# Mixer projections of a hybrid decoder trunk: high weights times both parts of the input in one 512-wide product, 256 columns at a time

## The chip, the cores and the metric

The kernel runs on one core of a Trainium2 chip. A core has a matrix engine (TensorE, PE in the profile, with its weight loads shown apart as PEld), a vector engine (VectorE, DVE), an engine for activations and copies (ScalarE, ACT), GpSimd (POOL) and SyncE (SP), which issues most DMAs here. The metric is the device time of one execution in microseconds. The time before is 1442.95 us, the median of three runs between 1440.83 and 1443.87 us.

## What is computed

Four pre-norm residual layers over a sequence of 256 positions, width 1024, in fp32. Each layer is a token mixer, an MLP with a squared ReLU and a gated projection of a per-layer input. Layers 0 and 3 mix by an S5 state space with a gated linear unit, layer 1 by forgetting attention (FoX), layer 2 by gated linear attention (GLA). Cut to the parts that matter here:

```python
# S5 (layers 0 and 3), after the scan
z = gelu(y) @ w_glu
z1, z2 = split(z, 2)                 # left gate, right gate
return (z1 * sigmoid(z2)) @ w_out
# FoX (layer 1)
proj = xn @ w_in                     # queries, keys, values (1024 each), 16 forget gates
o = softmax(q @ k.T * scale + forget_bias, causal) @ v
return o @ w_out
# GLA (layer 2)
proj = xn @ w_in                     # queries, keys (512 each), values, output gate r
o = chunked_linear_attention(q, k, v, gates)
return (norm(o) * gn_g * silu(r)) @ w_out
# every layer
h = h + mixer(rmsnorm(h))
h = h + square(relu(rmsnorm(h) @ w1)) @ w2
h = h + (p @ W_pp) * sigmoid(rmsnorm(h) @ W_pg)
```

## The kernel before

**Layout.** The residual stream lies transposed in SBUF, features on partitions and time along the row: `H[k]`, k = 0 to 7, each 128 x 256, two to a tile `HH[n]`. Weights stream from HBM once, in units of 512 KB.

**Two parts of each number.** A product is made from a high part (rounded to the fast format fp32r) and a low part (the rest) of both factors: high weights times high input, high weights times low input, low weights times high input. Inputs are kept as tiles of two row blocks, `x[k // 2][:, k % 2]`, with high and low part side by side, 256 columns each, so that both make one operand of 512 columns. `unit` (L187) loads raw weights (L171, three buffers), copies them into fp32r on ACT (`whi`, L179) and subtracts on DVE (`wlo`, L181), with four buffers for each part.

**Three ways to multiply.**
- `dense` (L202) takes 512 output columns at a time in two PSUM banks and goes through the input by units of 256 rows x 512 columns. `pairs` (L217) and `col` (L195) issue three products of 256 columns for each 128 x 128 block of weights: high x high, high x low, low x high (L198, L199, L200), all summed in the same 256 columns. One unit is 24 products. After four units the two banks are finished and handed to `evac`.
- `wide` (L226), used by the MLP, gives each 128 output columns a bank of its own: the high weights multiply both parts in one product of 512 columns (L234), the low weights the high part in one of 256 (L236). The bank then holds two halves, which `summed` (L241) adds: a copy of one half on ACT (L244) and an addition on DVE (L245).
- `rows` (L248) puts time on partitions, for the values of FoX and GLA and GLA's output gate.

**PSUM** has eight banks: three under the tag `acc`, three `wk`, one `po`, one `mk` (L22).

**Who uses dense.** FoX: queries (scaled by -0.125) and keys, for each half `cb` of the heads (L553, L554), both with `acc` alone; their `evac` (`augmented`, L511) multiplies with the row factor `r` straight from PSUM (L517). GLA: queries and keys (L632, L633); `query` multiplies PSUM into `e1`, `key` into `e2` and `e3`. S5: the left gate (L1106), whose `evac` multiplies with the sigmoid of the right gate (L1103) and splits the result into the two parts of `m`. `out_proj` (L293), the product by w_out at the end of each mixer, adds its banks to `HH[n]` (L296). Also the gate of the per-layer input (L473) and, through `pairs`, S5's right gate (L1253).

**What sets the order.** The program is written step by step, and the framework's scheduler (L1442) fixes the order on each engine when the program is built: it takes the earliest step in program order that its own timeline holds ready and for which a buffer is free. So PE's list interleaves steps: the attention parts of one half of FoX (scores L528, transposes L539, product with the values L548) stand among the queries and keys of the other half, and among the first units by w_out. Each engine then executes its list in order. In FoX, `o` has four tiles, one for each four heads (L565); in GLA four, two for each half of the value columns (L694).

Of the kernel before, what the change touches and what calls it, by code (L numbers as in the profile page):

```python
# [13 lines left out]
ALU = mybir.AluOpType  # L14
# [3 lines left out]
T, D, FF, DEPTH = 256, 1024, 4096, 4  # L18
# [42 lines left out]
class Trunk:  # L61
# [164 lines left out]
    def wide(self, ps, x, hi, lo, k, first, last):  # L226
# [3 lines left out]
        for n in range(4):  # L230
# [4 lines left out]
            for i in range(UK):  # L235
                self.last_mm = mm(ps[n][:, 0], lo[:, i, s], v[i][:, 0], start=False, stop=last and i == UK - 1, skip_group_check=True)  # L236

    def banks(self, tags):
        return [self.psum((128, 2, T), t) for t in tags]

# [52 lines left out]
    def out_proj(self, x, w):  # L293

        def evac(n, ps):
            self.nc.vector.tensor_tensor(self.HH[n], self.HH[n], ps, ALU.add)  # L296
        self.dense(x, w, evac, tags=("acc", "wk"))

    def log_sigmoid(self, *pairs):

# [188 lines left out]
    def fox(self, l):  # L489
        nc, A = self.nc, self.A  # L490
        NH, HD = 16, 64
        x = self.scaled(l)
        sq = self.squares()
        bf = self.small("bf", [NH, 1], bufs=1)
        self.load(bf, A["fox_bf"])
        f, e = (self.small(n, (NH, T), bufs=1) for n in ("w1", "w2"))
        rows = self.rstd_rows(sq)
        self.masks()
        r = self.rstd(rows)
        self.side(x, A["fox_wf"], f)  # L500
        nc.vector.tensor_tensor(f, f, r[0:NH], ALU.mult)
        nc.vector.tensor_scalar(f, f, bf, None, ALU.add)
        self.log_sigmoid((f, e))
        cf = self.a2("cf", (NH, 2, T))
        nc.gpsimd.memset(e, 1.0)
        nc.vector.tensor_tensor_scan(cf[:, 0], e, f, 0.0, ALU.mult, ALU.add)
        nc.vector.tensor_scalar(cf[:, 1], cf[:, 0], -1.0, None, ALU.mult)

        qk = [[self.t4("aug", (128, 2, 2, T)) for _ in range(4)] for i in range(2)]

        def augmented(i):  # L511
            def evac(n, ps):
                t = qk[i][n]
                nc.gpsimd.memset(t[HD:HD + 2], 1.0)
                nc.sync.dma_start(t[HD + 1 - i:HD + 2 - i].rearrange("x a b t -> x (a b) t"), cf[4 * n:4 * n + 4, 1 - i])
                for h in range(2):
                    nc.vector.tensor_tensor(t[0:HD, :, h], ps[h * HD:(h + 1) * HD], r[0:HD].unsqueeze(1).broadcast_to([HD, 2, T]), ALU.mult)  # L517
            return evac

        def weights(cb, half, heads):  # L520

            n, g = half + 1, len(heads)
            ps = self.psum((128, g, n * 128))
            m, z = self.small("m", [128, 4], bufs=3), self.small("z", [128, 4], bufs=3)
            s = self.t2("s", (128, g, n * 128))
            for i, h in enumerate(heads):
                q, k = (qk[j][cb * 2 + h // 4][0:HD + 2, h // 2 % 2, h % 2] for j in range(2))
                nc.tensor.matmul(ps[:, i], q[:, half * 128:(half + 1) * 128], k[:, :n * 128], start=True, stop=True)  # L528
            for i in range(g):
                nc.vector.tensor_tensor_reduce(s[:, i], ps[:, i], self.far[:, T - n * 128:], 1.0, 3.0e38, ALU.add, ALU.min, m[:, i:i + 1])  # L530
                nc.scalar.activation(s[:, i], s[:, i], AF.Exp, bias=m[:, i:i + 1], scale=-1.0, accum_out=z[:, i:i + 1])
            rz = self.small("rz", [128, 4], bufs=3)
            nc.vector.reciprocal(rz[:, :g], z[:, :g])
            for i in range(g):
                nc.vector.tensor_scalar(s[:, i], s[:, i], rz[:, i:i + 1], None, ALU.mult)
            pt = self.psum((128, g, n, 128), "mk")
            for i in range(g):
                for kb in range(n):
                    nc.tensor.transpose(pt[:, i, kb], s[:, i, kb * 128:(kb + 1) * 128], self.ident)  # L539
            pT = self.t2("pT", (128, g, n, 128))  # L540
            nc.scalar.copy(pT, pt)
            return pT

        def values(v, po, half, heads, pT):
            n = half + 1
            for kb in range(n):
                for i, h in enumerate(heads):
                    nc.tensor.matmul(po[(h % 2) * HD:(h % 2 + 1) * HD, h // 2 % 2, half * 128:(half + 1) * 128],  # L548
                                     v[:, kb, h * HD:(h + 1) * HD], pT[:, i, kb], start=kb == 0, stop=kb == n - 1)

        o = self.ktiles("o")
        for cb in range(2):
            self.dense(x, A["fox_w_in"][:, 0:D], augmented(0), (cb,), -0.125)  # L553
            self.dense(x, A["fox_w_in"][:, D:2 * D], augmented(1), (cb,))  # L554
            v = self.t4("v", (128, 2, 512), tag="c4")
            for quad in range(2):
                hs = list(range(quad * 4, quad * 4 + 4))
                parts = [(0, hs), (1, hs[:2]), (1, hs[2:])]
                pT = [weights(cb, *p) for p in parts]
                if quad == 0:  # L560
                    self.rows(x, A["fox_w_in"][:, 2 * D:], cb, lambda half, ps: nc.scalar.activation(v[:, half], ps, AF.Identity, scale=rows[:, half:half + 1]))
                po = self.psum((128, 2, T), "po")
                for i, p in enumerate(parts):
                    values(v, po, *p, pT[i])
                d = o[cb * 2 + quad]  # L565
                self.split(po, d[:, :, 0], d[:, :, 1])
        self.out_proj(o, A["fox_w_out"])

    def gla(self, l):
        nc, A = self.nc, self.A  # L570
        NH, DK, DV = 4, 128, 256
        x = self.scaled(l)
# [7 lines left out]
        rows = self.rstd_rows(sq)  # L580
        r = self.rstd(rows)
# [3 lines left out]
        y, e, cum = (self.t4(n, (128, NH, T)) for n in ("gy", "ge", "cum"))  # L585
        for h in range(NH):
            ps = self.psum((128, T))
# [13 lines left out]
        for h in range(NH):  # L601
            nc.scalar.activation(e1[:, h], cum[:, h], AF.Exp, scale=1.0 / 16.0)
            nc.scalar.activation(e2[:, h], cum[:, h], AF.Exp, scale=-1.0 / 16.0)
            c = slice(h, h + 1)
# [5 lines left out]
        v = [self.t4("v", (128, 2, 512), tag="c4") for half in range(2)]  # L610
        v = [[t[:, b] for b in range(2)] for t in v]
# [2 lines left out]

        def query(n, ps):
            e = e1[:, 2 * n:2 * n + 2]
            nc.vector.scalar_tensor_tensor(e, ps, DK ** -0.5, e, ALU.mult, ALU.mult)

        ku = [self.a2("ku") for _ in range(2)]

        def key(n, ps):
            n -= 2
            for e in (e2, e3):
                e = e[:, 2 * n:2 * n + 2]
                nc.vector.tensor_tensor(e, ps, e, ALU.mult)
            pt = self.psum((128, 2, 2, 128))
            for half in range(2):
                for i in range(2):
                    nc.tensor.transpose(pt[:, half, i], e3[:, 2 * n + i, half * 128:(half + 1) * 128], self.ident)
                nc.scalar.copy(ku[half].rearrange("p (h k) -> p h k", h=NH)[:, 2 * n:2 * n + 2], pt[:, half])  # L630

        self.dense(x, A["gla_w_in"], query, (0,))  # L632
        self.dense(x, A["gla_w_in"], key, (1,), tags=("acc", "wk"))  # L633
        state = [self.a2("state", (128, 2, DV)) for b in range(2)]
        os = [[None, None], [None, None]]
        att = []
# [11 lines left out]
        for half in range(2):  # L648
            at = att[half]
            for b in range(2):  # L650
                po = self.psum((128, 2, DV))
                for c in range(2):
# [4 lines left out]
                    for hh in range(2):  # L657
                        h = 2 * b + hh
# [6 lines left out]
                    for hh in range(2):  # L665
                        h = 2 * b + hh
                        nc.tensor.matmul(pu[:, hh, :], ku[half][cs, h * DK:(h + 1) * DK], v[half][b][cs, hh * DV:(hh + 1) * DV],
                                         start=True, stop=True)
# [421 lines left out]
    def s5(self, l):  # L1090
        nc, A = self.nc, self.A
        E = mybir.EngineType
        with nullcontext():
            steps = self.s5_start(l)
            with nullcontext():
                gT, last = steps()
        m = self.ktiles("glu", tag="m4")
        self.lo_after, self.raw_after = [last], self.last_unit
        for b, sg in enumerate(self.sg):

            def left(n, ps):
                t = sg[n % 2]
                nc.vector.tensor_tensor(t, ps, t, ALU.mult)  # L1103
                self.split(t, m[n][:, :, 0], m[n][:, :, 1])

            self.dense(gT, A["s5_w_glu"][l // 3], left, (b,), tags=("acc", "wk"))  # L1106
        self.lo_after, self.raw_after = [], None
        self.out_proj(m, A["s5_w_out"][l // 3])

# [336 lines left out]
```

## Time and profile before

| what | value |
|---|---|
| median of three runs | 1442.95 us (1440.83 to 1443.87) |
| the profiled execution | 1441.32 us |
| its span, first to last instruction | 1439.3 us |
| mean granted clock of TensorE | 0.993 |
| DVE busy | 1047.1 us, 1652 instructions |
| ACT busy | 719.5 us, 1118 instructions |
| DMA | 254.54 MB, mean 177 GB/s |

The stages follow one another. By the loads of their weights (SP's timeline), the MLP of layer 0 begins to load at 166 us, FoX's queries at 372, its w_out at 457 (last load at 482), the MLP of layer 1 at 487, GLA at 711, its w_out at 789 to 835, S5 of layer 3 at 1058, the last MLP at 1204.

How to read the rows. A group is "line engine operation output<-inputs shape xcount | busy us, mean ns of one | idle time before it and what ended it". A row of the timeline is "start us, us, engine line operation output<-inputs xcount". A row of the waits is "who waited <- for whom: us in total, times, longest". In the names, `acc`, `wk`, `po` and `mk` are PSUM banks, `whi` and `wlo` the parts of the weights. Products are pipelined in PE and their ends are modelled, so the duration of a product is longer than the distance to the next one's start. Some matmul records are missing.

### The profile page before, as it was taken

To read this page: it belongs to the slowest core of one execution; us is meant where nothing else is said; L and a number is where in the kernel's file an instruction comes from. 1 tells how busy PE (TensorE), PEld (TensorE's weight loads), DVE (VectorE), ACT (ScalarE), POOL (GpSimd) and SP (SyncE) were. 2 spreads that over 40 slices of the span, in tenths; PEclk is the share of its full clock that TensorE was granted. 3 is DMA by queue.
4 is the path that set the end of the run, shared out by engine and by line. 5 is a ranking of instruction groups with operands and counts; after the bars stand their busy time and mean duration, and the time that the engine had idled before them with its cause. 6 is when DMAs were issued, how large, how long until landed. Compare 5 with 4: busy or idle time off the path is not lost.

```text
span 1439.3 us, 26706 instructions
## 1 busy us (share of the span) xinstructions
PE 1396.7 (97%) x10818; PEld 1261.1 (88%) x10818; DVE 1047.1 (73%) x1652; ACT 719.5 (50%) x1118; POOL 100.6 (7%) x167
## 2 busy tenths in 40 slices
PE   9989999999999999999999999999997899999997
PEld 8888988889999888889988598888997799888897
DVE  9885678776866688897667468787676946766765
ACT  3233565454654655455567355445462345545543
POOL 3000000010010000000004000000003100000020
PEclk9999999999999999999999999999999999999999
DMA  9443656657554456766555256566656546556651
GB/s 297 111 120 108 180 171 196 189 183 238 171 157 136 122 167 193 248 226 211 196 161 170 94 153 196 195 215 197 205 162 210 172 152 181 179 183 194 188 189 59
DMA packets 143227, 254.54 MB, mean 177 GB/s; under 512 B 21648, under 2 KB 32240, under 8 KB 143104
## 3 DMA queue, kind: packets, MB, share of 16 engines
q1 hardware_dynamic: 129856, 227.66, 51.0%
q0 software_dynamic: 7360, 23.73, 4.8%
q10 hardware_dynamic: 5888, 1.44, 0.5%
q8 instruction: 84, 1.38, 0.4%
q14 instruction: 39, 0.32, 0.1%
HBM read 242.15 MB, written 7.86 MB: 174 GB/s over the span
## 4 chain that ended last, share of the span: by engine, by line
PE 63%; DMA 2%; DVE 2%; ACT 2%; issue 0%; DVEq 0%; POOLq 0%; ACTq 0%; SPq 0%
PE wk L234 9%; PE acc L234 7%; PE wk L236 4%; PE wk L198 4%; PE wk L199 4%; PE wk L200 4%; PE acc L198 4%; PE acc L199 3%; PE acc L200 3%; PE acc L236 3%; PE mk L234 3%; PE po L234 2%; PE mk L236 1%; PE acc L259 1%; PE acc L258 1%; PE acc L260 1%
## 5 line engine op out<-in xcount | busy, mean ns | idle before, releaser
L181 DVE TENSOR_TENSOR wlo<-raw,whi 128x1024 fp32r<-128x1024 f32 x404 | 492.0, 1226 | 276.2 <-ACT whi L179 274.6
L179 ACT CAST whi<-raw 128x1024 fp32r<-128x1024 f32 x404 | 420.8, 1049 | 489.4 <-DMA raw<-mlp_w 73.9
L234 PE MATMUL wk<-x,whi 128*128 128x512 f32 x576 | 181.3, 396 | 1.1 <-DVE relu L245 1.1
L236 PEld LDWEIGHTS wk<-x,wlo 128*128 128x128 f32 x576 | 106.8, 188 | 23.4
L234 PE MATMUL acc<-s,whi 128*128 128x512 f32 x384 | 119.2, 395 | 0.0
L236 PE MATMUL wk<-x,wlo 128*128 128x256 f32 x576 | 112.9, 279 | 0.0
L198 PE MATMUL acc<-x,whi 128*128 128x256 f32 x352 | 99.8, 287 | 1.8 <-DVE u L1166 1.0
L200 PE MATMUL acc<-x,wlo 128*128 128x256 f32 x352 | 99.9, 286 | 0.8 <-DVE wlo L181 0.8
L199 PE MATMUL acc<-x,whi 128*128 128x256 f32 x352 | 99.4, 285 | 0.0
L234 PEld LDWEIGHTS wk<-x,whi 128*128 128x128 f32 x576 | 90.3, 189 | 3.6 <-DVE relu L245 1.4
L236 PEld LDWEIGHTS acc<-s,wlo 128*128 128x128 f32 x384 | 71.0, 188 | 16.1
L234 PE MATMUL mk<-x,whi 128*128 128x512 f32 x256 | 81.5, 395 | 0.5 <-ACT whi L179 0.5
L236 PE MATMUL acc<-s,wlo 128*128 128x256 f32 x384 | 75.4, 280 | 0.0
L200 PE MATMUL wk<-s,wlo 128*128 128x256 f32 x256 | 72.4, 283 | 0.0
L199 PE MATMUL wk<-s,whi 128*128 128x256 f32 x256 | 72.4, 283 | 0.0
L198 PE MATMUL wk<-s,whi 128*128 128x256 f32 x256 | 72.4, 283 | 0.0
L198 PEld LDWEIGHTS acc<-x,whi 128*128 128x128 f32 x352 | 66.9, 191 | 3.3 <-issue 1.8
L200 PEld LDWEIGHTS acc<-x,wlo 128*128 128x128 f32 x352 | 67.2, 191 | 1.6 <-DVE wlo L181 1.3
L199 PEld LDWEIGHTS acc<-x,whi 128*128 128x128 f32 x352 | 67.2, 192 | 0.2
L234 PE MATMUL po<-s,whi 128*128 128x512 f32 x192 | 60.3, 395 | 0.0
L234 PEld LDWEIGHTS acc<-s,whi 128*128 128x128 f32 x384 | 59.1, 188 | 0.9
L234 PE MATMUL wk<-s,whi 128*128 128x512 f32 x192 | 59.1, 395 | 0.0
(404 smaller groups left out, 3362.9 us busy)
## 6 DMA issues: line engine op xcount, KB each, us to landing
raw<-mlp_w SPq DMA_DIRECT2D x256, 512.0 KB, 4.1
raw<-s_w_glu SPq DMA_DIRECT2D x32, 512.0 KB, 4.2
raw<-ple_gate SPq DMA_DIRECT2D x32, 512.0 KB, 3.6
raw<-fox_w_in SPq DMA_DIRECT2D x24, 512.0 KB, 3.8
raw<-gla_w_in SPq DMA_DIRECT2D x24, 512.0 KB, 4.6
raw<-s_w_out SPq DMA_DIRECT2D x16, 512.0 KB, 3.4
kept<-kept POOLq DMA_DIRECT2D x12, 512.0 KB, 4.7
raw<-s_w_in SPq DMA_DIRECT2D x11, 512.0 KB, 4.2
```

The costliest lines, as they stand in the source:

```text
L179: nc.scalar.copy(hi, raw)
L181: self.last_lo = nc.vector.tensor_tensor(lo, raw, hi.bitcast(F32), ALU.subtract)
L198: mm(ps, hi, x[:, 0], start=first, stop=False, skip_group_check=True)
L199: mm(ps, hi, x[:, 1], start=False, stop=False, skip_group_check=True)
L200: self.last_mm = mm(ps, lo, x[:, 0], start=False, stop=last, skip_group_check=True)
L234: mm(ps[n], hi[:, i, s], v[i], start=first and i == 0, stop=False, skip_group_check=True)
L236: self.last_mm = mm(ps[n][:, 0], lo[:, i, s], v[i][:, 0], start=False, stop=last and i == UK - 1, skip_group_check=True)
L258: mm(ps[half], a[:, 0, t], hi[:, k], start=k0 + k == 0, stop=False)
L259: mm(ps[half], a[:, 0, t], lo[:, k], start=False, stop=False)
L260: mm(ps[half], a[:, 1, t], hi[:, k], start=False, stop=k0 + k == nk - 1)
```

## The change

A new function `broad` computes 256 output columns at a time, with one bank for each 128 columns. A unit is now 512 rows x 256 columns: four row blocks (two input tiles), two banks. For each bank it issues four products of 512 columns with the high weights (both parts of the input) and then four of 256 columns with the low weights. Two units finish a group. `tags[n % 2]` gives the banks of a group. It takes the place of `dense` in `out_proj`, FoX's queries and keys, GLA's queries and keys and S5's left gate. Their `evac` functions first add the two halves of each bank: `summed` into a new tile `y`, or, in `out_proj`, two additions to each `H`.

```diff
+    def broad(self, x, w, evac, ns=range(4), scale=None, tags=("acc", "acc")):
+
+        mm = self.nc.tensor.matmul
+        for n in ns:
+            ps = self.banks([tags[n % 2]] * 2)
+            for k in range(0, 2 * len(x), 4):
+                hi, lo = self.unit(w[k * 128:(k + 4) * 128, n * 256:(n + 1) * 256], 4, 256, scale)
+                v = [x[(k + i) // 2][:, (k + i) % 2] for i in range(4)]
+                for c, p in enumerate(ps):
+                    s = slice(c * 128, (c + 1) * 128)
+                    for i in range(4):
+                        mm(p, hi[:, i, s], v[i], start=k == i == 0, stop=False, skip_group_check=True)
+                    for i in range(4):
+                        self.last_mm = mm(p[:, 0], lo[:, i, s], v[i][:, 0], start=False, stop=k > 0 and i == 3, skip_group_check=True)
+            evac(n, ps)
+
...
     def out_proj(self, x, w):
 
         def evac(n, ps):
-            self.nc.vector.tensor_tensor(self.HH[n], self.HH[n], ps, ALU.add)
-        self.dense(x, w, evac, tags=("acc", "wk"))
+            for h, p in zip(self.H[2 * n:2 * n + 2], ps):
+                for i in range(2):
+                    self.nc.vector.tensor_tensor(h, h, p[:, i], ALU.add)
+        self.broad(x, w, evac, tags=("acc", "wk"))
...
         def augmented(i):
             def evac(n, ps):
                 t = qk[i][n]
+                y = self.summed(self.t2("y", (128, 2, T)), ps)
...
                 for h in range(2):
-                    nc.vector.tensor_tensor(t[0:HD, :, h], ps[h * HD:(h + 1) * HD], r[0:HD].unsqueeze(1).broadcast_to([HD, 2, T]), ALU.mult)
+                    rows = slice(h * HD, (h + 1) * HD)
+                    nc.vector.tensor_tensor(t[0:HD, :, h], y[rows], r[rows].unsqueeze(1).broadcast_to([HD, 2, T]), ALU.mult)
...
-            self.dense(x, A["fox_w_in"][:, 0:D], augmented(0), (cb,), -0.125)
-            self.dense(x, A["fox_w_in"][:, D:2 * D], augmented(1), (cb,))
+            self.broad(x, A["fox_w_in"][:, 0:D], augmented(0), (2 * cb, 2 * cb + 1), -0.125)
+            self.broad(x, A["fox_w_in"][:, D:2 * D], augmented(1), (2 * cb, 2 * cb + 1))
...
         def query(n, ps):
             e = e1[:, 2 * n:2 * n + 2]
-            nc.vector.scalar_tensor_tensor(e, ps, DK ** -0.5, e, ALU.mult, ALU.mult)
+            y = self.summed(self.t2("y", (128, 2, T)), ps)
+            nc.vector.scalar_tensor_tensor(e, y, DK ** -0.5, e, ALU.mult, ALU.mult)
...
         def key(n, ps):
             n -= 2
+            y = self.summed(self.t2("y", (128, 2, T)), ps)
             for e in (e2, e3):
                 e = e[:, 2 * n:2 * n + 2]
-                nc.vector.tensor_tensor(e, ps, e, ALU.mult)
+                nc.vector.tensor_tensor(e, y, e, ALU.mult)
...
-        self.dense(x, A["gla_w_in"], query, (0,))
-        self.dense(x, A["gla_w_in"], key, (1,), tags=("acc", "wk"))
+        self.broad(x, A["gla_w_in"], query, (0, 1))
+        self.broad(x, A["gla_w_in"], key, (2, 3), tags=("acc", "wk"))
...
             def left(n, ps):
                 t = sg[n % 2]
-                nc.vector.tensor_tensor(t, ps, t, ALU.mult)
+                nc.vector.tensor_tensor(t, self.summed(self.t2("y", (128, 2, T)), ps), t, ALU.mult)
                 self.split(t, m[n][:, :, 0], m[n][:, :, 1])
 
-            self.dense(gT, A["s5_w_glu"][l // 3], left, (b,), tags=("acc", "wk"))
+            self.broad(gT, A["s5_w_glu"][l // 3], left, (2 * b, 2 * b + 1), tags=("acc", "wk"))
```

## The prediction

> **What bounds the kernel now.** I read the page's table of engines and the row of the core's span and granted clock first, then the list of waits on PE (TensorE), then the groups by form, and last the timeline of PE, because a busy PE in this profile need not be PE at its peak.
>
> ```profile
> PE 1396.7 (97%) x10818; PEld 1261.1 (88%) x10818; DVE 1047.1 (73%) x1652; ACT 719.5 (50%) x1118; POOL 100.6 (7%) x167
> ```
>
> ```profile
> core 0: 1439.3 us, clock 0.993
> ```
>
> PE is busy 1396.7 of 1439.3 us at nearly the full granted clock, and idles 42.6 us in all. DVE (VectorE, 73%) and ACT (ScalarE, 50%) have room. So the kernel ends when PE has worked through its list, and a change of PE's work counts in full unless it opens gaps. Of the gaps, most lie in S5's scan, which the change leaves alone; the list of waits has these two:
>
> ```profile
> PE acc L198 <- ACT o L274: 1.8, 2, 1.1
> PE po L548 <- ACT pT L541: 1.8, 2, 1.1
> ```
>
> They are at the joints the change touches: the product by w_out waiting for its late input `o` in FoX and GLA, and FoX's last attention parts. They are small now; the question is whether they stay small.
>
> **What one product costs.** The groups mislead:
>
> ```profile
> L234 PE MATMUL wk<-x,whi 128*128 128x512 f32 x576 | 181.3, 396 | 1.1 <-DVE relu L245 1.1
> ...
> L236 PE MATMUL wk<-x,wlo 128*128 128x256 f32 x576 | 112.9, 279 | 0.0
> ...
> L198 PE MATMUL wk<-s,whi 128*128 128x256 f32 x256 | 72.4, 283 | 0.0
> ```
>
> Three products of 256 columns at 283 ns (what `dense` does) against one of 512 at 396 and one of 256 at 279 (what the new `broad` does) looks like 174 ns saved each time, 100 us over 576 times. But 576 x 396 ns is 228 us where the group was busy only 181: the durations overlap. What counts is the distance between starts. In the timeline of PE (start, duration, operation), first S5's left gate by `dense`, then the MLP by `wide`, which already does what `broad` will do:
>
> ```profile
> 1172.85 0.28 PE L198 MATMUL acc<-g,whi 128*128 128x256 f32 x1
> ...
> 1184.37 0.28 PE L198 MATMUL wk<-g,whi 128*128 128x256 f32 x1
> ```
>
> ```profile
> 1271.34 0.63 PE L234 MATMUL acc<-s,whi 128*128 128x512 f32 x2
> ...
> 1274.13 0.63 PE L234 MATMUL acc<-s,whi 128*128 128x512 f32 x2
> ```
>
> ```profile
> 299.94 1.08 PE L234 MATMUL wk<-x,whi 128*128 128x512 f32 x4
> 300.86 0.64 PE L236 MATMUL wk<-x,wlo 128*128 128x256 f32 x4
> 301.33 0.63 PE L234 MATMUL wk<-x,whi 128*128 128x512 f32 x2
> ```
>
> The first pair spans 96 products (four units of 24) in 11.52 us: 120 ns each, 2.88 us a unit. The second spans one unit by `wide` (8 of 512, 8 of 256): 2.79 us. The third is four high then four low products in a row, exactly `broad`'s group: 1.39 us, two of them to a unit, 2.78 us. Both forms stream the same columns; a column costs a trifle less in the long form. So a unit saves 0.09 to 0.10 us, not 1.4; I take 0.095.
>
> **The parts of the change.**
>
> *Products removed.* Units of 512 KB, by the DMA issues:
>
> ```profile
> raw<-s_w_glu SPq DMA_DIRECT2D x32, 512.0 KB, 4.2
> ...
> raw<-fox_w_in SPq DMA_DIRECT2D x24, 512.0 KB, 3.8
> raw<-gla_w_in SPq DMA_DIRECT2D x24, 512.0 KB, 4.6
> raw<-s_w_out SPq DMA_DIRECT2D x16, 512.0 KB, 3.4
> ...
> raw<-s_w_in SPq DMA_DIRECT2D x11, 512.0 KB, 4.2
> ```
>
> Of s_w_glu the left half, 16; of fox_w_in queries and keys, 16; of gla_w_in queries and keys, 8; s_w_out 16; fox_w_out and gla_w_out 8 each: 72 units. 72 x 0.095 = 6.8 us less (6.5 to 7.2), all on the path, since PE is the path. PE loses 576 products and as many weight loads.
>
> The Trainium skill, page "TensorE: Matmul & The Clock Gate", section "Back-to-back issue gap", speaks against most of this: its table gives 262 cycles at 256 columns and 518 at 512, so the step follows the columns and a triple saves 6 cycles; by it the 576 triples would give an estimated 1.4 us. The trace disagrees: its step at 256 columns is 0.120 us, not 0.109. I keep 6.8, and hold a saving near nothing as a rival.
>
> *Loads.* A unit is now 512 rows by 256 columns, in runs of 1 KB where it had 2 KB. The s_w_in loads have that shape already: 4.2 us to landing against 3.4 to 4.6 for the others. Three units are in flight and a unit lasts 2.8 us: nothing, either way.
>
> *Evacuation.* The halves of a sum now lie in one bank side by side and must be added.
>
> ```profile
> L245 DVE TENSOR_TENSOR relu<-wk,relu 128x256 f32<-128x256 f32 x72 | 26.5, 415 | 2.1 <-ACT relu L244 2.1
> L244 ACT COPY relu<-wk 128x256 f32<-128x256 f32 x72 | 25.9, 369 | 12.0 <-PE wk L236 11.7
> ...
> L296 DVE TENSOR_TENSOR h<-h,acc 128x512 f32<-128x512 f32 x8 | 5.5, 685 | 2.5 <-PE acc L200 2.3
> ```
>
> Twenty groups of 256 columns (FoX 8, GLA 4, S5 8) gain two copies on ACT and two adds on DVE: 15 us of ACT, 17 us of DVE. Sixteen groups of w_out replace one add of 0.685 by four of about 0.415: 16 us of DVE. DVE goes to about 1080 us, ACT to 735: both still far below PE, hidden under it. The cover could fail at the banks. FoX uses only `acc`, three banks, two per group, so a group's second bank is the previous group's first, which PE left 1.39 us before that group ended and wants 1.39 us after: 2.78 us for a copy and an add of 0.37 + 0.415. One weight cast ahead on each engine would make it 3.1:
>
> ```profile
> L181 DVE TENSOR_TENSOR wlo<-raw,whi 128x1024 fp32r<-128x1024 f32 x404 | 492.0, 1226 | 276.2 <-ACT whi L179 274.6
> L179 ACT CAST whi<-raw 128x1024 fp32r<-128x1024 f32 x404 | 420.8, 1049 | 489.4 <-DMA raw<-mlp_w 73.9 <-PE wk L199 71.2 <-PE acc L199 68.9
> ```
>
> I take nothing; at worst 0.3 us at six joints, 1.8 us. Against that, GLA's query sums leave their banks before `e1` is ready, where the old ones waited: possibly a gain below a microsecond.
>
> *The order of the inner dimension.* This is the cost that matters. `dense` goes through all four row blocks of an input for 512 columns, so the last quarter of the input is first needed at the fourth unit, and the other 512 columns can be worked up to the same point: six of the eight units by w_out do without the last input tile. `broad` needs all of the input by its second unit. Without the last tile it can do: the first unit of groups 0 and 1 (2 x 2.78), the two third-tile products per bank of their second units (8 x 0.233 = 1.9), and, as only one `acc` bank is left, half of group 2's first unit (1.39): 8.8 us instead of 6 x 2.88 = 17.3. In FoX the last tile is late:
>
> ```profile
> L198 PE MATMUL acc<-o,whi x32: 278/283/384, 476.9 to 508.5; 128*128 128x256 f32 x32
> ```
>
> ```profile
> 504.09 0.66 PE L548 MATMUL po<-pT,v 128*64 128x128 f32 x8 [1.11 <-ACT pT L541]
> 505.43 0.51 PE L198 MATMUL acc<-o,whi 128*128 128x256 f32 x2 [0.68 <-ACT o L274]
> ```
>
> From 476.9 on (first start in the first row) the products by w_out are what PE does between the last attention parts; at 504.1 and 505.4 it has run out of them and waits. The six units are done by then, and the two that need the last tile remain. After the change 8.5 us of that filling is missing. If the attention chain kept its length, all 8.5 would become idle PE. But the chain is itself held up by its filling:
>
> ```profile
> ACT pT L541 <- PE mk L539: 5.9, 3, 2.5
> ```
>
> In 474 to 506 us (waits of ACT) the copies of turned probabilities waited 5.9 us for PE's transposes, which stand in PE's queue behind those products. The chain also may begin earlier: the first four heads of a half need only the first of two groups of queries and keys, which now is done two units (5.6 us) before the second. I take 1.5 us for FoX, near the end where the chain shortens; bounds -2 (it also removes the 1.8 us of idle time) to +8.5.
>
> In GLA the same joint:
>
> ```profile
> 828.73 0.51 PE L198 MATMUL acc<-o,whi 128*128 128x256 f32 x2 [1.10 <-ACT o L274]
> ```
>
> ```profile
> L275 DVE TENSOR_TENSOR o<-wk,o x8: 414/418/425, 826.1 to 835.7; 128x256 fp32r<-128x256 f32 x8
> ```
>
> The old first unit uses only the first tile; the new wants the second after 0.47 us, while `o` is still being split in pieces until 836.1. Filling by first-tile products of three or four banks covers about 1.5 us. I take 0.8 us, bounds 0 to 2.
>
> In S5 (layers 0 and 3) the last left group is split just before w_out starts (timeline of DVE, layer 0):
>
> ```profile
> 157.56 1.43 DVE L1103 TENSOR_TENSOR sg<-wk,sg 128x512 f32<-128x512 f32 x2
> ...
> 160.40 1.28 DVE L275 TENSOR_TENSOR glu<-sg,glu 128x512 fp32r<-128x512 f32 x2
> ```
>
> The second multiplication (the later half of 1.43) starts with the last product done, at 158.3, and the last split part ends at 161.7: 3.4 us; a copy and an add make it about 4, and the second unit wants it after 2.78 + 0.47 = 3.2 us. Group 1's first unit fills 2.78 us. I take 0.2 us a layer, bounds 0 to 1.
>
> The sum: -6.8 + 1.5 + 0.8 + 0.4 = -4.1 us. PE's order is fixed when the program is built, from a timeline of the framework's own, so a new mixture of instructions also moves things that no row shows; the range has to carry that.
>
> The profiled execution took 1441.32 us (span 1439.3), inside the three runs (1440.83 to 1443.87) and 1.6 below their median. 1441.3 - 4.1 = 1437.2 on its basis, 1438.9 on the median's. A change within 0.2%, 2.9 us, can't be told from none here: the three runs alone spread 3.0 us.
>
> **The rivals.**
>
> *The missing filling costs more than the products save (slower).* FoX's chain keeps its length: +8.5; GLA at its bound +2, S5 +0.4; with -6.8 that is +4.1 us, 1447.0. It decides from the point where the joints idle 6.8 us together. For it: the chain's order on ACT and DVE is fixed too. Against it: the 5.9 us above. Chance 0.18.
>
> *Half of it.* FoX's joint costs 4 to 5, the others as taken: about -1.3 us, 1441.6, no change to be told. Chance 0.20.
>
> *The pace belongs to the place, not to the form.* If PE takes 120 ns for every 256 columns in these stages, a long product costs 240, a triple 360 as before, nothing is saved and the joints cost their 2.7 us: 1445.7, still within 0.2%. For it: no row shows the long form outside the MLP. Against it: the clock is the same in both and every operand has the same type; chance 0.06. The page's rule above, that columns alone count, would leave it 1.4 us better.
>
> *Everything is filled.* The early heads remove FoX's idle time as well: -6.8 - 1.8, 1434.4. Chance 0.14.
>
> *My forecast* has 0.42: -3 to -6 us.
>
> **How the numbers follow.** Faster: 0.42 + 0.14 = 0.56. Same: 0.20 + 0.06 = 0.26. Slower: 0.18. The range takes the full gain without joints at its low end (1434) and at its upper end reaches the slower case's own figure (1447): half of that case (0.09) and most of the filled one (0.1) lie outside. The likeliest case alone spans 1437 to 1440.
>
> **What would show it.** PE's count should fall to 10242. In the new line of 512 columns, groups of four high and four low products should start 1.39 us apart, a unit 2.78; a unit of 2.85 would speak for the third rival. The waits of PE on `o` (ACT, L274's split) and on `pT` should total 4 to 7 us in FoX and GLA; over 10 us there proves the slower rival, under 2 the best case. No wait of a `broad` product on an evacuation of its bank above 0.3 us. PE's idle time outside these joints should be as before; if it is not, the rebuilt order and not the change itself is the cause, and I am wrong in the step that leaves the rest alone.

## The result and the profile after

The kernel after takes 1473.79 us (median of 4, 1471.89 to 1484.82; the highest had a granted clock of 0.967, the others 0.978 to 0.981) beside 1443.41 us before: ratio 1.0235, 95% interval 1.0208 to 1.0262. It is 30 us slower; the forecast was 4 us faster, and the range ended at 1447. The first page row and the row of span and clock, after:

```profile
PE 1406.8 (96%) x10242; PEld 1239.8 (84%) x10242; DVE 1075.9 (73%) x1740; ACT 734.7 (50%) x1158; POOL 97.0 (7%) x167
```

```profile
core 0: 1472.3 us, clock 0.981
```

Three things changed: PE has 576 products less and yet is busy 10 us longer; it is idle 1472.3 - 1406.8 = 65.5 us, where it was 42.6; and its mean granted clock fell from 0.993 to 0.981. DVE and ACT are where the prediction put them. The list of waits on PE names the new idle time (total, times, longest; the rows left out fall within S5, and the list before has them too):

```profile
PE mk L559 <- DVE s L555: 6.6, 3, 2.3
PE acc L274 <- DVE y L261: 5.5, 1, 5.5
...
PE acc L249 <- DVE x L382: 2.4, 2, 2.0
PE wk L297 <- DVE o L706: 2.1, 1, 2.1
PE wk L198 <- ACT shl L290: 2.0, 1, 2.0
PE wk L369 <- DVE diag L368: 2.0, 1, 2.0
```

Only the fourth line belongs to a joint that the prediction named (GLA's `o`). The pace of the products is nearly as forecast (1.39): a group of four long and four short products, start to start, takes 1.41 us (timeline of PE):

```profile
415.98 1.09 PE L249 MATMUL acc<-x,whi 128*128 128x512 f32 x4
416.91 0.64 PE L251 MATMUL acc<-x,wlo 128*128 128x256 f32 x4
417.39 0.86 PE L249 MATMUL acc<-x,whi 128*128 128x512 f32 x3
```

To see where the time went I took lengths of stages from the traces, between the starts of the norms' products by `ones`: FoX from the norm before its own to the one after it (375.9 to 551.3 us before), GLA from its norm to the next (747.6 to 892.7), S5's layer 0 from the start to the end of its w_out, layer 3 from its norm to there. In us:

| kernel | S5, 0 | FoX | GLA | S5, 3 | span |
|---|---|---|---|---|---|
| before | 181.3 | 175.4 | 145.1 | 126.6 | 1439.3 |
| after | 179.2 | 196.8 | 156.1 | 128.5 | 1472.3 |

FoX lost 21.4 us and GLA 11.0; S5's layer 0 gained 2.1. A profile of FoX's middle, in stretches of time, first before, then after (bounds and length, busy time of PE, PEld, DVE, ACT, POOL; the last three numbers are granted clock, DMA share, GB/s):

```profile
425.00:476.00 51.00, 50.38 (x372) 45.98 (x370) 33.32 (x89) 29.70 (x66) 1.84 (x2) 1.00 0.49 140
```

```profile
405.00:425.00 20.00, 20.00 (x108) 16.65 (x107) 13.90 (x22) 11.49 (x17) 0.73 (x3) 0.89 0.36 104
425.00:476.00 51.00, 44.81 (x246) 37.26 (x245) 31.20 (x82) 26.39 (x60) 1.84 (x2) 0.93 0.43 125
...
500.00:535.00 35.00, 30.82 (x173) 25.14 (x173) 21.72 (x57) 18.88 (x39) 0.00 (x0) 0.85 0.34 105
```

PE stands still there, and for a while after it works again it is granted less. The timelines of PE and of ACT, after, at the end of FoX's first half:

```profile
455.13 0.63 PE L559 MATMUL mk<-ident,s 128*128 128x128 f32 x4 [2.35 <-DVE s L555]
458.10 1.09 PE L559 MATMUL mk<-ident,s 128*128 128x128 f32 x4 [2.34 <-DVE s L555]
460.60 2.08 PE L249 MATMUL acc<-x,whi 128*128 128x512 f32 x4 [1.41 <-DVE y L261]
```

```profile
459.23 0.59 ACT L561 COPY pT<-mk 128x512 f32<-128x512 f32 x1 [1.86 <-PE mk L559]
459.71 0.93 ACT L260 COPY y<-acc 128x256 f32<-128x256 f32 x3
```

All three `acc` banks hold second-half queries, finished at 451.3; the copies that would empty them come 8 us later, three in a row, directly behind the last `pT` (the copy of the transposed probabilities) of the first half. ACT waited 1.86 us just before, with those copies ready. At the start of FoX the same: three copies in a row directly behind `shl` (403.34 us). `shl` (the forget gates' weights), `s` (the scores), `pT` and the new `y` all come from the ten `s2` buffers. That gave the first theory: **R**, the destination of the copies holds them up, if buffers are handed out in program order. Its rivals: **J**, the prediction's slower case, w_out's missing filling; **B**, banks that turn over twice as often. In the experiments a stop is a stretch in which PE stands still.

### The profile page after: what moved, and what is told of

The parts are those of the page before. It is cut to its first block, busy times and chain, and to the rows that moved or that the text cites. A ratio compares the mean times of both kernels' runs of the same rounds, so it can differ in the third digit from the quotient of the medians.

```text
span 1472.3 us, 25690 instructions
## 1 busy us (share of the span) xinstructions
PE 1406.8 (96%) x10242; PEld 1239.8 (84%) x10242; DVE 1075.9 (73%) x1740; ACT 734.7 (50%) x1158; POOL 97.0 (7%) x167
## 4 chain that ended last, share of the span: by engine, by line
PE 76%; issue 11%; DVE 6%; DMA 3%; ACT 2%; POOL 1%; DVEq 0%; POOLq 0%; SPq 0%; ACTq 0%
PE wk L234 9%; PE acc L234 8%; PE acc L249 5%; PE wk L236 5%; PE acc L236 4%; PE wk L198 4%; PE wk L199 4%; PE wk L200 4%; PE mk L234 3%; PE wk L249 3%; PE po L234 3%; PE acc L198 2%; PE acc L251 2%; PE acc L199 2%; PE acc L200 2%
## 5 line engine op out<-in xcount | busy, mean ns | idle before, releaser
L234 PE MATMUL acc<-x,whi 128*128 128x512 f32 x192 | 58.8, 396 | 0.0
L236 PEld LDWEIGHTS mk<-x,wlo 128*128 128x128 f32 x256 | 47.6, 188 | 10.2
L198 PE MATMUL acc<-x,whi 128*128 128x256 f32 x192 | 54.3, 287 | 1.8 <-DVE u L1188 1.0
L249 PE MATMUL acc<-x,whi 128*128 128x512 f32 x176 | 51.3, 410 | 3.8 <-DVE x L382 2.4
L200 PE MATMUL acc<-x,wlo 128*128 128x256 f32 x192 | 53.9, 283 | 0.6 <-DVE wlo L181 0.6
L199 PE MATMUL acc<-x,whi 128*128 128x256 f32 x192 | 54.0, 285 | 0.0
```

The lines of the kernel that those rows point to most:

```text
L198: mm(ps, hi, x[:, 0], start=first, stop=False, skip_group_check=True)
L199: mm(ps, hi, x[:, 1], start=False, stop=False, skip_group_check=True)
L200: self.last_mm = mm(ps, lo, x[:, 0], start=False, stop=last, skip_group_check=True)
L234: mm(ps[n], hi[:, i, s], v[i], start=first and i == 0, stop=False, skip_group_check=True)
L249: mm(p, hi[:, i, s], v[i], start=k == i == 0, stop=False, skip_group_check=True)
```

## The experiments

Ratios are to the kernel before on the same chip, with the 95% interval; stage lengths are from each one's profile. FoX, where it is as before, took 175.1 to 175.7 us in eight other profiles (177.2 in e13), GLA 145.1 to 145.7 in five; the order-only kernel run twice gave 177.4 and 177.5, 146.1 and 145.6. So a difference of two or three microseconds in these stages means something.

### FoX: where the copies go, and which products need them

e1, the whole change with one word more:

```
-                y = self.summed(self.t2("y", (128, 2, T)), ps)
+                y = self.summed(self.t2("y", (128, 2, T), tag="g2"), ps)
```

> The whole change, but FoX's added half sums `y` go to the two `g2` buffers, which nothing else uses in FoX, and not to the ten `s2` buffers, which the softmax's `s` and `pT` and `shl` share. Theory R (the destination of the copies: `s2` buffers are handed out in the order of the program, so a group's evacuation stands behind the last `pT` of the half before and behind `shl`, and TensorE runs out of banks): FoX's three stops around the norm (2.0, 2.0, 2.0 us) and the three in its middle (2.3, 2.3, 1.4 us) go, and the granted clock there returns to 1.0; FoX falls by 12 to 18 us, the kernel to 1456 to 1462 us. Rival J (the missing filling at w_out, the order of the inner dimension): nothing changes before the tail, 1470 to 1475 us. Rival B (bank turnover by itself: two banks a group of three, a copy and an add each): stops remain at every group, 1466 to 1474 us.

Measured: 1461.01 us, ratio 1.0143 (1.0099 to 1.0187), FoX 184.7. The copies now stand between the exponentials of the first half (timeline of ACT), and FoX's middle is full at full clock:

```profile
436.35 0.19 ACT L551 ACTIVATION_READ_ACCUMULATOR s<-s,m 128x1 f32 x1
436.73 0.37 ACT L260 COPY y<-acc 128x256 f32<-128x256 f32 x1 [0.19 <-PE acc L251]
...
439.78 0.37 ACT L260 COPY y<-acc 128x256 f32<-128x256 f32 x1 [1.03 <-PE acc L251]
442.78 0.59 ACT L561 COPY pT<-mk 128x512 f32<-128x512 f32 x1 [2.63 <-PE mk L559]
```

```profile
425.00:476.00 51.00, 51.00 (x301) 42.64 (x300) 37.03 (x94) 30.18 (x64) 2.44 (x3) 1.00 0.54 165
```

R holds for 12.1 of FoX's 21.4 us. One stop of 2.0 us at the start stayed: the second unit of the first query group needs the third input tile (`x`, L382), which `dense` needed only 5.8 us into its work.

e2 does only FoX's queries and keys by `broad`, with `s2`; e7 the same with `g2`; e11 only the keys and e15 only the queries, both with `g2`. The diff of e11 to the kernel before (e15 the other way round):

```
-            self.dense(x, A["fox_w_in"][:, D:2 * D], augmented(1), (cb,))
+            self.broad(x, A["fox_w_in"][:, D:2 * D], augmented(1), (2 * cb, 2 * cb + 1))
...
+                y = self.summed(self.t2("y", (128, 2, T), tag="g2"), ps) if i else ps
```

> Only FoX's queries and keys by `broad`, with copies into `s2` as in the change; the left gate, GLA and every w_out as before. R: the stops around the norm and in the middle stay, 1457 to 1465 us. J: no loss, as w_out is as before: 1442 us (16 units at 0.095 us less).

> Only FoX's queries and keys by `broad`, with the sums in the `g2` buffers. R (the copies' buffers were all of that part's loss): 16 units x 0.095 = 1.5 us saved, 2.0 us lost where the second unit waits for the last gains of the input: 1442 to 1445 us. If the turnover of the banks costs too: 1447 us or more.

> FoX's keys alone by `broad`, sums in `g2`; its queries by `dense`. Theory X (what e7 lost, 6.8 us, began at the input: the second unit needed the last gains 2.0 us too early, and the stop was paid again in a slower granted clock): no such stop, 1442 to 1445 us. Rival T (it was lost in the tail, where the attention parts fall into another order and stop 1.4 and 1.5 us): 1447 to 1452 us.

> FoX's queries alone by `broad`, sums in `g2`; keys by `dense`. If the queries lose what e7 lost (they stop 2.0 us at the input and move the attention parts of the tail): FoX 6 to 9 us longer, 1447 to 1451 us. If it takes both (the four groups share three banks): FoX 0 to 3 us longer, 1441 to 1445 us.

| kernel | median | ratio | FoX |
|---|---|---|---|
| e2, both, `s2` | 1461.58 | 1.0134 (1.0113 to 1.0156) | 195.7 |
| e7, both, `g2` | 1450.23 | 1.0043 (1.0029 to 1.0056) | 184.3 |
| e11, keys, `g2` | 1443.69 | 1.0010 (0.9999 to 1.0021) | 175.7 |
| e15, queries, `g2` | 1449.47 | 1.0047 (1.0031 to 1.0062) | 180.5 |

e2 shows that w_out isn't needed for the loss: J is out as the main cause. From e2 to e7 the buffers alone give 11.4 us back. Of the 8.9 us that stay, the queries alone make 5.1 and the keys 0.3, and the two together 3.5 more; e15's stage falls between its two cases.

PE's first product by w_out divides the stage. After the change it is this one (before, the first start is 476.9):

```profile
493.51 0.82 PE L249 MATMUL acc<-o,whi 128*128 128x512 f32 x2
```

| kernel | FoX up to there | from there on |
|---|---|---|
| before | 101.0 | 74.3 |
| after | 119.0 | 77.9 |
| e1, the change with `g2` | 101.1 | 83.7 |
| e2, both, `s2` | 119.6 | 76.1 |
| e7, both, `g2` | 101.0 | 83.3 |

So where the copies' buffers do their harm they cost 18 us, and `g2` gives all of it back; but the tail behind, only 2 to 4 us too long with `s2`, is then 9 us too long, and the 12.1 and 11.4 us are what is left of the gain. In e7's tail there are stops of 1.4 and 1.5 us between attention parts that stand in another order. So e11 gave the time that theory X (the loss begins at the stop for the input) expected, but its reason was wrong. Why this order is worse stays open.

### GLA: four attempts at one stop

e3 does only GLA's queries and keys by `broad`.

> Only GLA's queries and keys by `broad`; all else as before. Theory D (the add of a query group stands in VectorE's order behind the multiplication by `e1`, which waits for GpSimd; the product by rows waits 5.5 us for that bank): 1448 to 1452 us, with one stop of about 5 us ahead of the values. J (GLA's loss is w_out's): 1442 to 1443 us.

Measured: median 1463.84 us, ratio 1.0131 (1.0096 to 1.0166), GLA 155.7: all of GLA's loss but 0.4 us. The profile is of the fastest of four runs, 1454.25 us at a granted clock of 0.986; the other three took 1463 to 1465 us at 0.975 to 0.979, and where they lost the further 9 to 11 us no trace shows. The stop, and what follows it (timeline of PE; then the stretch 779 to 785 us before, clock 1.00, and in e3, clock 0.53):

```profile
778.87 0.76 PE L274 MATMUL acc<-whi,x 128*128 128x512 f32 x1 [5.54 <-DVE y L261]
780.00 0.80 PE L275 MATMUL acc<-wlo,x 128*128 128x512 f32 x1 [0.36 <-DVE wlo L181]
780.59 0.63 PE L276 MATMUL acc<-whi,x 128*128 128x512 f32 x1
781.02 0.63 PE L274 MATMUL acc<-whi,x 128*128 128x512 f32 x1
```

```profile
779.00:785.00 6.00, 6.00 (x29) 4.92 (x28) 6.00 (x8) 2.77 (x3) 4.00 (x3) 1.00 0.68 193
```

```profile
779.00:785.00 6.00, 5.63 (x14) 4.08 (x15) 4.16 (x5) 1.99 (x5) 6.00 (x7) 0.53 0.68 181
```

The products for the values (L274 to L276) start 427 ns apart instead of 231. Theory **D** blamed DVE's order: the add that frees the bank stands behind the multiplication by `e1`, which waits 1.9 us for GpSimd. e5 gives both key groups `wk` banks, so that the values find `acc` free:

```
-        self.broad(x, A["gla_w_in"], key, (2, 3), tags=("acc", "wk"))
+        self.broad(x, A["gla_w_in"], key, (2, 3), tags=("wk", "wk"))
```

> As the run with only GLA's queries and keys by `broad` (e3, span 1452.5), but both key groups take `wk` banks, so that the products for the values find `acc` banks that the first query group left. Theory D (the stop of 5.5 us is one add in VectorE's order behind a multiplication that waits for GpSimd): the stop goes and the clock after it holds, span 1440 to 1446 us. Rival (the loss in GLA is the longer chain of sums, whatever the banks): stop stays or moves to another product, 1450 to 1455 us.

Measured: 1455.23 us, ratio 1.0079 (1.0057 to 1.0101), GLA 155.7, no gain in the stage. The bank's stop is gone and a weight cast's has come (waits of PE, GLA):

```profile
PE acc L274 <- ACT whi L179: 4.6, 1, 4.6
```

D fails: the wait named was one of several that end at about the same time. Next suspect, **Q**: the copies of the query groups, which in ACT's order put the exponentials of `cum` behind the second logarithm, and so late. e9 takes the queries out (keys alone, `wk`), e10 the keys (queries alone); e9 against e5:

```
-        self.broad(x, A["gla_w_in"], query, (0, 1))
+        self.dense(x, A["gla_w_in"], query, (0,))
```

> GLA's keys alone by `broad` (both groups in `wk`), its queries by `dense`; all else as before. Theory Q (moving the stop from an add to a weight cast showed that no single wait is to blame: the copies of the query groups stand in ScalarE's order in the middle of the gate's chain of exponentials and logarithms, which then runs late and holds up the casts behind it): with no query copies there, no stop, 1442 to 1444 us. Rival L (the longer way of a group's sums through two engines and the wait of the keys' second group): 1447 to 1455 us.

> GLA's queries alone by `broad`, its keys by `dense`. Q: the chain is late as in e5 (the exponentials of `cum` start near 26 us after the norm instead of 20), but the keys' 11.5 us of products now lie ahead of the values; what is lost is between 1 and 9 us, 1444 to 1452 us, more than in e9. L: less than in e9.

Measured: e9 1.0053 (1.0037 to 1.0068), GLA 152.4; e10 1.0044 (1.0030 to 1.0058), GLA 150.3. In e9 the order of the exponentials is as before, and 2.9 us of stop are there all the same:

```profile
PE acc L274 <- ACT whi L179: 2.9, 1, 2.9
```

The queries alone lose less than the keys alone, against Q and for its rival L (a group's sums take a longer way), so Q is at most a part. What holds the queries up in e10 (5.2 us) was not followed further. What e9 and e5 share: before the values PE has 32 key products (5.7 us), where `dense` had 96 short ones (11.5 us). Four key banks don't fit into `wk` (three), so the second group waits. Theory **K**: the form holds two banks where `dense` holds one, and so halves the work that can be open while the gate's chain fills ACT. e14 gives the second group two banks that GLA leaves unused:

```
-            ps = self.banks([tags[n % 2]] * 2)
+            ps = self.banks([tags[n % 2]] * 2 if isinstance(tags[n % 2], str) else tags[n % 2])
...
+        self.broad(x, A["gla_w_in"], key, (2, 3), tags=("wk", ("po", "mk")))
```

> As e9 (GLA's keys alone by `broad`), but the second key group takes `po` and `mk`, which GLA leaves unused, so that all 64 key products can run ahead of the values as the 96 of `dense` did. Theory K (the form holds two banks where `dense` holds one, so only half as much work can be open when the gate's chain holds up ScalarE): no stop at the values, GLA as before less 0.4 us, the kernel 1441 to 1443 us. Rival: the copies and adds of the keys delay the casts whatever the banks, 1446 us or more.

Measured: GLA 146.8, 5.6 us less than e9, with no stop at the values and one of 2.5 us at the transposed keys (waits of PE, GLA):

```profile
PE wk L646 <- DVE e L642: 2.5, 1, 2.5
```

K holds for the keys in this stage. The kernel does not bear it out: at 1.0027 (1.0015 to 1.0038) its median is 1446.83 us, above the expected 1441 to 1443 and inside the rival's "1446 us or more". The stage explains 1.7 of the 3.8 us. The profile is of the fastest of nine runs (1443.69 us, clock 0.993); the other eight had 0.987 to 0.989, and no trace shows where.

e13 is e3 with 32 products of ones in the stop, to hold the clock:

```
+                with self.tc.issue_after(self.last_mm.ins):
+                    for _ in range(32):
+                        nc.tensor.matmul(warm, self.ones, self.ones, start=True, stop=True)
```

> As e3 (only GLA's queries and keys by `broad`, a stop of 5.5 us ahead of the values, then about 13 products at 427 ns instead of 231), with 32 extra products of a matrix of ones put into that stop, about 4.6 us of work whose result nothing reads. Theory C (after a stop the clock is granted at half for some 5 us, so a stop costs about one and a half times its length): the products after the stop keep 231 ns a step, GLA is 2 to 3 us shorter than in e3 although more is done. If the slow products were due to anything that comes with the values themselves (their weights, their banks): no change, or up to 4.6 us longer.

Measured: 1.0089 (1.0076 to 1.0103), GLA 160.0, 4.3 longer than e3. The rebuilt order let only three products for the values follow before the transposed keys, which wait for `e3` (timeline of PE):

```profile
778.46 0.48 PE L274 MATMUL acc<-whi,x 128*128 128x512 f32 x1
778.78 0.39 PE L275 MATMUL acc<-wlo,x 128*128 128x512 f32 x1
779.01 0.40 PE L276 MATMUL acc<-whi,x 128*128 128x512 f32 x1
786.03 0.66 PE L652 MATMUL wk<-ident,e 128*128 128x128 f32 x2 [6.63 <-DVE e L648]
786.35 2.06 PE L249 MATMUL wk<-x,whi 128*128 128x512 f32 x4
```

As a remedy it failed. For theory C (after a stop the clock is granted at half) it speaks all the same: behind the filling the values step by about 0.23 us, and behind the new stop the products are slow (four in 1.85 us), whatever they are.

### w_out: the order or the banks

e4 does only w_out by `broad`, in all four mixers. e8 takes its order of units, but the short products and one bank to a group:

```
+        for n in range(4):
+            ps = self.psum((128, 2, T), ("acc", "wk")[n % 2])
+            for k in range(0, 8, 4):
+                hi, lo = self.unit(w[k * 128:(k + 4) * 128, n * 256:(n + 1) * 256], 4, 256)
...
+                        self.col(ps[:, c], x[(k + i) // 2][:, (k + i) % 2], hi[:, i, s], lo[:, i, s], k == i == c == 0, k > 0 and i == 3)
```

> Only the products by w_out by `broad`, in all four mixers; queries, keys and the left gate as before. J at the prediction's price (8.5 us in FoX, 2 in GLA, 0.4 in S5, less 3.0): 1451 us. The prediction's own step (1.5 + 0.8 + 0.4 - 3.0): 1443 us. R and D: most of the change's 30 us is not here, 1441 to 1448 us.

> No long products at all. Only the order of the units by w_out is the new one (512 rows by 256 columns, a group's second half needing the last input tile), with the three products of `dense` and one bank to a group instead of two. Theory O (the order alone loses FoX's filling): as e4 without its 3.0 us of products, 1450 to 1454 us. Theory K (two banks to a group lose it: four groups could be open, with two banks each only two and a half): 1442 to 1445 us.

Measured: e4 1449.98 us, 1.0049 (1.0032 to 1.0066), FoX 181.2, GLA 146.1. e8 1444.58 us, 1.0007 (0.9997 to 1.0017), FoX 177.4, GLA 146.1. In FoX, before the last stop for `o`, the kernel before had done 144 of 192 products by w_out (17.3 us), e4 and the change 50 of 128 (8.8 us), e8 120 of 192 (14.4 us). The rows of these stops, e4 and then e8 (the one of before stands in the prediction):

```profile
501.01 1.22 PE L249 MATMUL acc<-o,whi 128*128 128x512 f32 x2 [1.41 <-DVE o L291]
```

```profile
503.81 0.39 PE L198 MATMUL acc<-o,whi 128*128 128x256 f32 x1 [0.69 <-ACT o L290]
```

So the order alone costs FoX 2.0 us. e4 differs from e8 in its long products and its four additions too; the counts point to the doubled banks, K again, but no run takes these apart. In e4's tail the clock is 0.78 around the last stop (stretch 500 to 512 us; before, 1.00):

```profile
500.00:512.00 12.00, 10.99 (x55) 9.74 (x56) 8.58 (x16) 5.49 (x7) 0.00 (x0) 0.78 0.30 85
```

### S5, and what can be kept

e6 keeps `broad` in S5 alone (left gate and s_w_out); e12 adds GLA's keys as in e9, e16 as in e14. `out_proj` takes a flag: `dense` and the single add for FoX and GLA, `broad` for S5.

```
-        self.out_proj(m, A["s5_w_out"][l // 3])
+        self.out_proj(m, A["s5_w_out"][l // 3], broad=True)
```

> Only S5: the left gate and s_w_out by `broad` (32 of the 72 units). The product price of the prediction (0.095 us a unit) with little lost at the joint: 3.0 us less, less 0.4 for the joints: 1440.0 to 1441.5 us. If the pace belonged to the place: 1443 to 1444 us.

> S5's left gate and w_out by `broad` (as e6) and GLA's keys by `broad` in `wk` (as e9). If the parts add and Q holds: 1440.3 - 0.4 = 1439.9 us, 1439 to 1441 us. If L holds: 1444 us or more.

> S5's left gate and w_out by `broad` (e6) and GLA's keys in four banks (e14). If K holds: 3.2 + 0.4 us below the kernel before, ratio 0.997 to 0.998. If not: 1445 us or more.

Measured: e6 1440.27 us, ratio 0.9975 (0.9963 to 0.9986), faster than both kernels: 3.2 us for 32 units, 0.10 a unit (0.06 to 0.17 by the interval). e12 1.0051 (1.0038 to 1.0063), with GLA at 152.4 as in e9, against Q once more. e16 1.0032 (1.0020 to 1.0043), a miss: its GLA is 146.7, 1.6 us more than e6's, but it is 7 us slower than e6, and the rest lies in stages with the same instructions, 2.9 of it in S5's layer 3. That stage, unchanged in most kernels, took 126.2 to 132.4 us; two repeats were to tell whether the program sets it.

> The kernel before, unchanged, profiled a second time; in the first its S5 part of layer 3 (from the norm to the end of w_out) took 126.6 us. If the program's order sets that time: 126 to 127 us again. If the execution does: anywhere from 126 to 132 us.

> The order-only kernel (e8), unchanged, profiled a second time; in the first its S5 part of layer 3 took 132.4 us. If the program's order sets it: 132 to 133 us again. If the execution does: some other value from 126 to 132 us.

e18 took 128.2 us there where e8 had 132.4: at least 4 us belong to the execution, not to the program. The granted clock over the stage differs with it, 0.93 and 0.91 (0.96 in the 126.6 us of the kernel before). That does not explain e16: its 131.0 us had 0.95, e6's 128.1 had 0.93. e17 answers nothing: that one execution of the kernel before took 3497 us (below). What e16 loses outside GLA stays open.

## Why the prediction was wrong, point by point

*What bounds the kernel; pitch, not duration.* Right, and a little too high. PE remains the path, with the 10242 products that were forecast. In S5 of layer 3, after the change, 16 units in a row take 44.85 us (1206.92 to 1251.77), 2.80 each where `dense` took 2.88: 0.08 us a unit against 0.095 taken, 5.5 us instead of 6.8 over 72 units. e6's 0.10 a unit agrees within its interval. By the Trainium skill's table, in which the step follows the columns (page "TensorE: Matmul & The Clock Gate", section "Back-to-back issue gap"), an estimated 0.6 of the 1.4 us would have been left in e6, which measured 3.2, at least 2.0 by its interval.

*Loads.* Nothing, as taken: none of PE's waits after is put down to a load of these matrices.

*Evacuation.* Here it failed: "I take nothing; at worst 0.3 us at six joints, 1.8 us." The engine time was right to 4 us (DVE 1075.9, ACT 734.7). But the step compared durations, as if a copy began when its group ended, and its sign, no wait of a `broad` product on an evacuation above 0.3 us, was broken by one of 1.4. Two questions were not asked. Where does the copy go: into buffers that the softmax also draws on, which put it behind the whole attention of the half before; 18 us up to w_out, 11 to 12 us net (e1, e2 against e7). And where does it stand, with how many banks held meanwhile: that is shown for GLA's keys (e14: 5.6 us back of the 7.3 that e9 lost). The rest is only located: 5.2 us with GLA's queries (e10), and FoX's remaining 8.9 us in the tail, with its queries (e15).

*The order of the inner dimension.* The account of the filling was exact, 8.8 us of work for 17.3. The price was too low: 1.5 us taken for FoX; e4's stage is 5.8 longer, 6.6 with the 0.8 us of products that the forecast held saved, inside the bounds of -2 to 8.5 and nearer to the rival's end. GLA's 0.8 us was 1.8 (e4: 1.0 longer, 0.8 saved). And e8 shows that most of it is not the order; the banks, which the step had used only in passing ("as only one `acc` bank is left"), are the likely rest. Nor does this price come on top of the others: FoX takes 184.7 us in e1, with w_out by `broad`, and 184.3 in e7 without. S5's joints were small, as taken.

*Idle time counts once.* The sum took this without saying so. FoX's five stretches from 366 to 535 us, each with its missing clock, come to 0.03 x 39 + 0.11 x 20 + 0.07 x 51 + 0.15 x 35 = 12 us; before, all were granted 1.00. Some of that falls into the stops themselves, so 12 is an upper estimate of what the clock added to FoX.

*The rivals.* The slower one was the right side by the wrong way: its mechanism is worth e4's 6.6 us, not 30. Its sign did not come either: PE's waits on `o` and `pT` in FoX (1.4 and 0.9 us) and on `o` before GLA's w_out (2.1) make 4.4 us, where over 10 was to prove it and 4 to 7 was the forecast's own. "PE's idle time outside these joints should be as before; if it is not, the rebuilt order and not the change itself is the cause" named the sign but mistook its meaning: e1 and e14, which alter nothing but buffers and banks, show that part of it is the change's own doing. That the range should "carry" such moves, while nothing in it did, is the second fault.

## What to carry to other kernels

A form of the product that needs twice the accumulator banks can halve the work that stands open in front of a late input (32 products for 96 in GLA, 5.7 us for 11.5); count that work at every stall of the neighbouring chain, not only the pace of the products. Follow each new copy to its destination: whose buffers are they, and who takes them before it in the program. And where removing one named wait only brings up another, ask what was running there before, and no longer is.

## What the runs showed of the hardware

*A stop can be paid twice.* After PE had stood 5.54 us (e3), nine of the next products for the values started 426 or 427 ns apart, then about 230 again; in the kernel after, two stops of 1.99 us with 0.67 us of work between, and only products of one column just ahead, left 24 short products at 0.21 us each instead of 0.12 (timeline of PE, the first three):

```profile
403.48 0.39 PE L198 MATMUL wk<-x,shl 128*16 128x256 f32 x1 [1.99 <-ACT shl L290]
403.68 0.41 PE L199 MATMUL wk<-x,shl 128*16 128x256 f32 x1
403.89 0.41 PE L200 MATMUL wk<-x,shl 128*16 128x256 f32 x1
```

A single stop of 1.96 us can go either way. In the kernel after it was not followed by slow products; in e1, at the same place, ten long products behind it took 3.94 us, 0.39 each (clock 0.50 from 394 to 397 us), and in e2 and e7 about as long. The first row is of the kernel after, the other two of e1:

```profile
392.88 1.66 PE L249 MATMUL acc<-x,whi 128*128 128x512 f32 x6 [1.96 <-DVE x L382]
```

```profile
393.09 4.13 PE L249 MATMUL acc<-x,whi 128*128 128x512 f32 x10 [1.96 <-DVE x L382]
397.03 0.80 PE L251 MATMUL acc<-x,wlo 128*128 128x256 f32 x4
```

The Trainium skill, page "TensorE: Matmul & The Clock Gate", Part 1, tells of half the clock after an idle window of some 3.4 us and gives 426.7 ns for 512 columns in that state. The 427 ns agree; here a stop well below that length was enough, in some executions.

*One execution at another pace.* e17, the kernel before, has full granted clock by its row and yet the long products last 830 ns where they lasted 396 (its group on the page), over the whole span. Its trace holds no record of the clock at all, where that of the first execution holds ten; so a granted clock of 1.000 is no proof of full pace.

```profile
core 0: 3495.2 us, clock 1.000
```

```profile
L234 PE MATMUL wk<-x,whi 128*128 128x512 f32 x576 | 409.5, 830 | 0.0
```

*A stage that varies by itself.* S5's layer 3 took 132.4 and 128.2 us in two executions of one program, at a granted clock of 0.91 and 0.93, so single profiles say nothing there below 4 us.
